# Two layers of a hybrid RWKV-7, attention and Fourier backbone: the recurrence's inverse and key products in other places of the program, with projections put in fixed places between them

## The chip, the cores and the metric

The kernel runs on one core of one Trainium2 chip. The time is device microseconds (us) of one execution, the median of three runs. Beside it stands one profiled execution, which has a time of its own. A core has five engines that run in parallel, each through its own program in order: PE (matrix products; its weight loads are shown as PEld), DVE (elementwise), ACT (activations and copies), POOL (elementwise), and SP, which issues DMA transfers.

## The reference

```python
SEQ, CTX_LEN, D_MODEL, DEPTH = 512, 256, 1024, 2
for l in range(DEPTH):
    a  = modulate(rms_norm(h, norm_mix_pre[l]), m[0], m[1])
    ac = modulate(rms_norm(hc, norm_mix_pre[l]), mc[0], mc[1])
    u_r, u_q, u_k, u_v, u_f, u_g = _split(a @ w_in[l], IN_SIZES)
    c_r, c_q, c_k, c_v, c_f, c_g = _split(ac @ w_in[l], IN_SIZES)
    yr_c, yr, ... = rwkv_branch(c_r, u_r, ...)          # recurrence over 256 context and 512 latent tokens
    ya = windowed_attention(q, k, v, k_c, v_c, attn_sink[l])
    mix = merge_branches(yr, ya, fourier_mix(u_f), u_g, ...)   # gated by sigmoid(u_g)
    h = h + m[2] * rms_norm(mix, norm_mix_post[l])
    ...                                                  # then a gated ConvFFN
def step(S, inp):                                        # the recurrence, both directions, 4 heads of 64
    r_t, w_t, k_t, v_t, kk_t, b_t = inp
    sa = jnp.einsum("bhvk,bhk->bhv", S, -kk_t)
    S = S * w_t[:, :, None, :] + sa[..., :, None] * b_t[..., None, :] + v_t[..., :, None] * k_t[..., None, :]
    return S, jnp.einsum("bhvk,bhk->bhv", S, r_t)
```

## The kernel before, in words

Each of the two layers has a mixing stage (input projection, recurrence, attention, Fourier mixing, gates) and an FFN stage. The change touches the recurrence of the mixing stage and the projections that run beside it.

**Projections.** One projection of 128 columns is three passes of fp32r products over the 1024 inputs (`gemm3`, lines 177, 178, 179 of the kernel before): 24 products over the 512 latent tokens and, where context is wanted, 24 over the 256 context tokens. Layer 0 wants both nearly everywhere, so a projection there is mostly 48 products; in layer 1 most are 24. Its weights come from `wload`: a DMA of `wr`, a rounding to `wh` on ACT, and the rest `wl` on DVE or POOL (line 118); these tiles are rings that turn in the order in which the code asks for them. Besides the nine projections that the recurrence needs there are eight others (K, V, two of Fourier, four of Q, stored to DRAM in `zd`, those of K and Q after a rotation on PE, DVE and POOL), and gate projections, of which `AHEAD` = 12 are asked for ahead of the Fourier part. Their results are in tile `mm`, so `mm` stands for these projections in the rows.

**Recurrence.** The 768 tokens of a layer are cut into 12 chunks of 64, taken in six pairs (w = 0 to 5; 0 and 1 are context), both directions at once. For each pair there are these parts:
- *Features*, `wkv_features`: two low-rank products on PE (line 814), activations on ACT, and scans and products on DVE and POOL (lines 726 to 855), and at its end the *key products* on PE (line 864) with two masks after each (`MR` and `W`, lines 869 and 870 on DVE), and `BK` times a decay on POOL (line 872).
- *Inverse*, `wkv_inverse`: a triangular inverse. Its first part is on DVE: a transpose (909), fifteen rounds of two small operations (917, 919; called the triangle here), and two transposes (929, 930). Its second part, the *merge*, is on PE in five groups of small products (938, 944, 948, 967, 974), with copies on DVE and ACT between them.
- *Two steps*, `wkv_prep` and `wkv_step`: transposes (987, 997), then q0 (1021 and a copy 1024), its product with the inverse (1028, copy 1031 to `XV`), the state's update (1039, and the addition 1042 to `ZV`), and the outputs (1047, 1052).

**Order.** All of the recurrence is emitted in `tc.high_priority()`. The eight other projections and the gates are emitted after it, at lower priority, and a list scheduler puts them on each engine wherever the recurrence leaves room. So in the program before, products of `mm` stand between nearly all groups of the recurrence, and the inverse of the next pair stands on DVE between the operations of the pair before it. After the recurrence comes its readout (`rwkv_readout`), then the Fourier part, with the gates that are left (in layer 0 about 270 products of gates come after the last step, beside the readout).

Of the kernel before, what the change touches and what calls it, by code (L numbers as in the profile page):

```python
# [16 lines left out]
TL = 512  # L17
TC = 256
TT = TL + TC
# [9 lines left out]
ATT_SCALE = 0.125  # L29
# [4 lines left out]
QC = 1152  # L34
KC = QC + 512
VC = KC + 128
FC = VC + 128
# [17 lines left out]
RING = ((5, 3, 3), (8, 4, 6))  # L55

AHEAD = 12
FOUR = 1
RATE = ((1, 1, 0), (1, 1, 1, 2))

# [3 lines left out]
class Kern:  # L64
# [292 lines left out]
    def advance(self, bg, n):  # L357
        for _ in range(n):
            if bg is None or next(bg, self) is self:
                return  # L360

    def gains(self, l, which, G=None, k0=0, n=KD):

        v = 1 if which == "mix" else 4
        row = V_NMIX if which == "mix" else V_NFFN
        if G is None:
            G = self.t(self.cp, [128, KD, 2], f"G{l}{which}")
        self.nc.vector.scalar_tensor_tensor(
            G[:, k0:k0 + n], self.mT[l][:, 8 * v + k0:8 * v + k0 + n], 1.0,
            self.V1[l][:, row + k0:row + k0 + n].unsqueeze(2).broadcast_to((128, n, 2)), ALU.add, ALU.mult)  # L370
        return G, self.mT[l][:, 8 * (v - 1):8 * (v - 1) + 8]
# [406 lines left out]

    def wkv_features(self, l, w, F, P, wp, wt):

        nc = self.nc
        x = P["x"]
        NC = 2
        WT = NC * CH
        W = {}
        MR = self.t(wp, [128, 4 * NC, 128], "MR", bufs=2)
        need_y = l == 0 or w > 1
        m = 128 if need_y else 64
        first = w in (0, 2, 3)
        part = "c" if w < 2 else "l"  # L790
        los = (w * WT, TC - (w + 1) * WT) if w < 2 else ((w - 2) * WT, TL - (w - 1) * WT)
        base = TL if w < 2 else 0

        def rows(t, h):
            return t[64 * h:64 * h + 64]

        for d in range(2):
            lo = base + los[d]

            def flip(s):  # L800
                return s[:, :, ::-1] if d else s
# [29 lines left out]
            e1 = self.t(wp, [128, 2, NC, CH + 1], "e1", bufs=4)  # L831
# [13 lines left out]
            BK = self.t(wp, [128, NC, 2, 128], "BK", bufs=4)  # L845
# [10 lines left out]
            vs = self.t(wp, [128, 2, WT + CH], "vs_", bufs=4)  # L856
            nc.gpsimd.memset(vs[0:64, :, 0:64], 0.0)
            nc.gpsimd.memset(vs[64:128, :, WT:WT + 64], 0.0)
            self.act(vs[0:64, :, 64:64 + WT], tok(F["v"])[0:64])
            self.act(vs[64:128, :, 0:WT], tok(F["v"])[64:128])  # L860
            for h in range(2):
                ps = self.ps()
                for q in range(4):
                    nc.tensor.matmul(ps[:, q * 128:q * 128 + m], lhsT=BK[:, q // 2, q % 2, :],
                                     rhs=W1[h][:, q // 2, q % 2, 0:m], start=True, stop=True)
                pv = ps.rearrange("p (q t) -> p q t", q=4)[:, :, 0:m]
                oth = 1 - h
                mask = lambda z: rows(self.gmask, z)[:, 0:m].unsqueeze(1).broadcast_to((64, 4, m))
                nc.vector.tensor_tensor(rows(MR, h)[:, 4 * d:4 * d + 4, 0:m], rows(pv, h), mask(h), ALU.mult)
                nc.vector.tensor_tensor(rows(W1[h], oth).rearrange("p c k t -> p (c k) t")[:, :, 0:m], rows(pv, oth),  # L870
                                        mask(oth), ALU.mult)
            nc.gpsimd.tensor_tensor(
                BK, BK, e1[:, :, :, 64].rearrange("p k c -> p c k").unsqueeze(3).broadcast_to((128, NC, 2, 128)), ALU.mult)
            W[d] = (W1, BK, vs, e1)
        return w, W, MR, los

    def wkv_scan(self, l, win, then, F, S, wb):
        nc = self.nc
        w, W, MR, los = win
        NC = 2  # L880
        TTt = self.wkv_inverse(MR, wb)
        cur = S["cur"]
        if cur is None:
            cur = self.wkv_prep(0, W, wb)
            for h in range(2):
                nc.gpsimd.memset(cur[0][h][64 * h:64 * h + 64], 0.0)
        for j in range(NC):
            nxt = None
            if j + 1 < NC:
                nxt = self.wkv_prep(j + 1, W, wb)  # L890
            elif then is not None:
                nxt = self.wkv_prep(0, then[1], wb)
            self.wkv_step(l, w, j, F, W, MR, TTt, cur, nxt, wb, los)
            cur = nxt
        S["cur"] = cur

    def wkv_inverse(self, MR, wp):


        nc = self.nc  # L900
        mm = nc.tensor.matmul
        NI = 8
        Fm = self.t(wp, [128, 16, 32], "iv", bufs=3)
        F16 = self.t(wp, [128, 16, 16], "F16", bufs=1)
        T = self.t(wp, [128, 16, 16], "T16", bufs=1)
        tmp = self.t(wp, [128, 64], "itmp", bufs=1)
        m0, m1, r1 = (self.lmask[:, z:z + 1] for z in (0, 1, 2))
# [6 lines left out]
        for q in range(15):  # L914
            n, m = 15 - q, q + 1
# [11 lines left out]
        TTt = self.t(wp, [128, NI, 64], "TTt", bufs=2)  # L927
        Tn = self.t(wp, [128, NI, 64], "iv", bufs=3)
        nc.vector.transpose(Tn.rearrange("q i (b t) -> q t b i", b=4), X2)
        nc.vector.transpose(TTt.rearrange("q i (b t) -> q t b i", b=4), X1)  # L930

        Ps = self.t(wp, [128, NI, 16], "Ps", bufs=1)
        pp = self.ps()
# [41 lines left out]
                   tile_position=(o + 32, o))  # L975
        self.act(TTt[0:32, :, 32:64], pa[1][0:32])
        nc.vector.tensor_copy(TTt[64:96, :, 32:64], pa[1][64:96])
        return TTt

    def wkv_prep(self, j, W, wp):  # L980

# [347 lines left out]
    def mix(self, l, at, atp, W, pls, ring, A, B):  # L1329

        nc, tc, I = self.nc, self.tc, self.I
        ctx = l == 0
        n = TT if ctx else TL
        w_in = I["w_in"][l]
        colw = lambda c: self.wload(w_in[:, c:c + 128])
        rp = self.pool("rp", side=B)
        P = self.rwkv_params(l, rp)
        F = {m: self.t(rp, [128, 2, TT], m) for m in ("r", "k", "v")}
# [7 lines left out]
        for j, c in enumerate(COLS):  # L1346

            wide = ctx or c not in (0, 1, 8)
            if j < len(W):
                pl, pc = pls[j], self.proj(W[j], at, lat=False, ctx=wide)[1]  # L1350
                if j == len(W) - 1 and ring is not None:
                    ring.release()
            else:
                pl, pc = self.proj(colw(c * 128), at, ctx=wide)
# [10 lines left out]
        wa = self.pool("wa", side=B)  # L1365
        wt = self.pool("wt", bufs=6, side=B)
        wb = self.pool("wb", side=B)
        S = {"cur": None}
        with tc.high_priority():
            w0 = self.wkv_features(l, 0, F, P, wa, wt)  # L1370
            w1 = self.wkv_features(l, 1, F, P, wa, wt)
            self.wkv_scan(l, w0, w1, F, S, wb)

        stg = self.pool("stg", bufs=2 + l, side=B)
        cos = self.t(stg, [128, TL], "cos", bufs=1)
        nc.sync.dma_start(out=cos, in_=self.C["c_cos"])
        sin = self.t(stg, [128, TL], "sin", bufs=1)
        nc.sync.dma_start(out=sin, in_=self.C["c_sin"])
        stores = []
        cols = [(KC, 1), (VC, 1), (FC, ctx), (FC + 128, ctx)] + [(QC + 128 * j, ctx) for j in range(4)]  # L1380
        for j, (c, wide) in enumerate(cols):
            t = self.t(stg, [128, TT], "stg")
            pl, pc = self.proj(self.wload(w_in[:, c:c + 128]), at, ctx=wide)
            sc = {} if j < 4 else dict(scale=ATT_SCALE)
            self.act(t[:, :TL], pl, **sc)
            if wide:
                self.act(t[:, TL:], pc[:, :TC], **sc)

            def store(j=j, t=t, m=TT if wide else TL):
                if j == 0 or j > 3:  # L1390
                    self.rope(t, cos, sin, stg)
                nc.sync.dma_start(out=self.zd[l][j, :, :m], in_=t[:, :m])

            stores.append(store)
            if len(stores) > l:
                stores.pop(0)()
        for store in stores:
            store()
        stg.release()


# [49 lines left out]
        work = fill()  # L1451
        with tc.high_priority():
            for w in range(2, 7):
                w0, w1 = w1, self.wkv_features(l, w, F, P, wa, wt) if w < 6 else None
                self.wkv_scan(l, w0, w1, F, S, wb)
            wb.release()
            wt.release()
            wa.release()
            tmp = self.pool("rtmp", side=B)
            self.rwkv_readout(l, F, P, y, tmp)  # L1460
            tmp.release()
# [20 lines left out]
        def back(j, wide=True):  # L1482
            t = self.t(fp, [128, TT], "back", bufs=3)
            m = TT if wide else TL
            nc.sync.dma_start(out=t[:, :m], in_=self.zd[l][j, :, :m])
            return t

        for _ in range(AHEAD):
            self.advance(work, 1)
            self.advance(bg, MODS[l][0])  # L1490
        self.banks(dict(x=3), dict(s=1, v=2, a=1))
# [2 lines left out]
        vt = self.values_layout(back(1), vp)  # L1494
        self.fourier(z, ctx, fp, lambda: (self.advance(work, FOUR), self.advance(bg, MODS[l][1])))
        yf = [pair(t) for t in z]
# [311 lines left out]
```

## Time and profile before

| what | value |
|---|---|
| median of three runs | 2505.8 us (2498.93 to 2506.62) |
| the profiled execution, its own time | 2513.85 us |
| its span in the profile | 2511.9 us |
| PE busy | 2293.3 us, 91% of the span |
| DVE busy | 1889.0 us, 75% |
| ACT, POOL busy | 1052.8 us (42%), 965.1 us (38%) |

All times in rows are from the start of the profiled execution's span. Busy time of an engine in a stretch is time in which at least one of its instructions ran. PEclk is the share of TensorE's full clock (2.4 GHz) that was granted, 0.5 being 1.2 GHz. In layer 0 the recurrence with what lies around it runs from about 143 to 508 us, in layer 1 from about 1539 to 1860 us.

### The profile page before, as it was taken

The page shows a single profiled execution, that of the slowest core. Times are in us where ns is not written, and L with a number is a line of the kernel's source. Part 1 is how long each engine was busy: PE and PEld are TensorE (multiplying, and loading weights), DVE is VectorE, ACT ScalarE, POOL GpSimd, SP SyncE. Part 2 cuts the span into 40 slices and gives each one's busy share as a digit, 9 for nine tenths or more (in the row PEclk, how much of TensorE's full clock was granted, in tenths as well). Part 3 has the DMA queues.
Part 4 walks back from the last instruction along what each step waited for, and adds up shares of the span by engine and source line. Part 5 has one row for each costly group of instructions (what it writes and reads, how often), then busy time and mean ns, then how long its engine had stood idle before and what let it go on. Part 6 is the DMA issues. An engine that isn't in the chain of part 4 may idle for free. (4 is left out here: it accounts for less than half of the span.)

```text
span 2511.9 us, 43604 instructions
## 1 busy us (share of the span) xinstructions
PE 2293.3 (91%) x16612; PEld 1923.1 (77%) x16612; DVE 1889.0 (75%) x3458; ACT 1052.8 (42%) x2153; POOL 965.1 (38%) x965
## 2 busy tenths in 40 slices
PE   7878999999999979999999989889889997899997
PEld 4757777887777768898898777667667776888886
DVE  4967777838866587778778854888667857989988
ACT  3234343335434444343333544435345434544443
POOL 4443322023332363333333544343224424644453
PEclk9989989999999989999999999899999998999999
DMA  7611111644334322222222322112275643322321
GB/s 241 190 51 47 57 37 46 204 146 122 118 122 125 104 67 65 63 72 68 64 69 66 122 93 63 54 59 61 76 211 149 195 128 113 117 88 85 98 89 59
DMA packets 284529, 251.36 MB, mean 100 GB/s; under 512 B 14524, under 2 KB 241300, under 8 KB 284320
## 3 DMA queue, kind: packets, MB, share of 16 engines
q1 hardware_dynamic: 284320, 248.58, 32.0%
q8 instruction: 131, 2.15, 0.4%
q14 instruction: 78, 0.64, 0.1%
HBM read 221.23 MB, written 27.29 MB: 99 GB/s over the span
## 5 line engine op out<-in xcount | busy, mean ns | idle before, releaser
L177 PE MATMUL mm<-at,wh 128*128 128x256 f32 (+2 forms) x1968 | 661.8, 337 | 14.4 <-DVE v L614 7.0
L178 PE MATMUL mm<-at,wh 128*128 128x256 f32 (+2 forms) x1968 | 660.5, 336 | 12.8 <-POOL at L118 7.3
L179 PE MATMUL mm<-at,wl 128*128 128x256 f32 (+2 forms) x1968 | 659.7, 336 | 8.2 <-DVE wl L118 5.9
L118 POOL TENSOR_TENSOR wl<-wr,wh 128x512 fp32r<-128x512 f32 (+1 forms) x248 | 341.8, 1385 | 466.2 <-ACT wh L106 444.0
L177 PEld LDWEIGHTS mm<-at,wh 128*128 128x128 f32 x1968 | 380.8, 194 | 46.9 <-issue 5.6
L178 PEld LDWEIGHTS mm<-at,wh 128*128 128x128 f32 x1968 | 381.1, 194 | 43.4 <-POOL at L118 10.0
L179 PEld LDWEIGHTS mm<-at,wl 128*128 128x128 f32 x1968 | 380.9, 194 | 34.4 <-DVE wl L118 8.9
L106 ACT ACTIVATE wh<-wr 128x512 fp32r<-128x512 f32 (+1 forms) x342 | 204.9, 605 | 235.2 <-PE mm L178 141.3
L118 DVE TENSOR_TENSOR wl<-ws,wh 128x512 fp32r<-128x512 f32 x176 | 166.8, 949 | 65.6 <-ACT wh L106 65.6
L177 PE MATMUL x<-dh,hid 128*128 128x512 f32 x440 | 178.0, 405 | 29.8 <-DVE acc L604 27.7
L295 DVE SCALAR_TENSOR_TENSOR ma<-mw,s,ma 128x256 f32<-128x256 f32 x336 | 187.3, 597 | 11.0 <-DMA mw<-in_mod_w 8.2
L179 PE MATMUL x<-dh,hid 128*128 128x512 f32 x440 | 173.3, 395 | 1.0 <-DVE hid L118 1.0
L178 PE MATMUL x<-dl,hid 128*128 128x512 f32 x440 | 173.2, 394 | 0.0
L604 DVE TENSOR_TENSOR acc<-x,acc 128x512 f32<-128x512 f32 x200 | 134.4, 682 | 24.2 <-PE x L179 23.7
L118 POOL TENSOR_TENSOR dl<-dr,dh 128x1024 fp32r<-128x1024 f32 x44 | 112.2, 2549 | 83.9 <-ACT dh L106 83.9
L106 ACT ACTIVATE wh<-ws 128x512 fp32r<-128x512 f32 x170 | 103.7, 623 | 84.9 <-PE mm L178 70.5
L177 PEld LDWEIGHTS x<-dh,hid 128*128 128x128 f32 x440 | 83.3, 189 | 56.4 <-DVE acc L604 38.6
L154 POOL TENSOR_TENSOR ws<-wr,wr 128x512 f32<-128x512 f32 x42 | 66.4, 1580 | 139.5 <-DVE wl L118 136.9
L178 PE MATMUL x<-at,wh 128*128 128x512 f32 (+2 forms) x312 | 114.4, 367 | 5.0 <-POOL at L118 3.1
L177 PE MATMUL x<-at,wh 128*128 128x512 f32 (+2 forms) x312 | 114.7, 368 | 0.9 <-DVE wh L114 0.7
L106 ACT ACTIVATE P<-P,st 128x513 f32<-128x513 f32 (+5 forms) x120 | 86.0, 722 | 69.8 <-DVE P L1234 58.6
L154 POOL TENSOR_TENSOR ws<-ws,wr 128x512 f32<-128x512 f32 x42 | 62.8, 1495 | 132.5 <-DVE wl L118 75.0
(490 smaller groups left out, 4859.0 us busy)
## 6 DMA issues: line engine op xcount, KB each, us to landing
mw<-in_mod_w SPq DMA_DIRECT2D x96, 512.0 KB, 4.1
wr<-in_ffn_up SPq DMA_DIRECT2D x176, 256.0 KB, 3.1
wr<-in_w_in SPq DMA_DIRECT2D x164, 256.0 KB, 3.0
dr<-in_ffn_down SPq DMA_DIRECT2D x44, 512.0 KB, 3.3
gd<-sg SPq DMA_DIRECT2D x32, 256.0 KB, 2.0
wraw<-in_w_out SPq DMA_DIRECT2D x32, 256.0 KB, 3.7
hd<-h SPq DMA_DIRECT2D x32, 256.0 KB, 2.4
h<-hd SPq DMA_DIRECT2D x28, 256.0 KB, 6.7
```

Source lines behind the costliest of these rows:

```text
L106: return self.nc.scalar.activation(out, in_, func, **kw)
L118: e.tensor_tensor(lo, full, hi.bitcast(F32), ALU.subtract)
L154: e.tensor_tensor(raw[m], raw[x], raw[y], op)
L177: mm(ps, lhsT=lh, rhs=rh, start=first and k == 0, stop=False)
L178: mm(ps, lhsT=lh, rhs=rl, start=False, stop=False)
L179: mm(ps, lhsT=ll, rhs=rh, start=False, stop=last and k == nk - 1)
L295: nc.vector.scalar_tensor_tensor(acc[s], mw[:, k % 4], v, acc[s], ALU.mult, ALU.add)
L604: nc.vector.tensor_tensor(acc[i][:, cs], ps, acc[i][:, cs], ALU.add)
```

## The change

1. `wkv_features` is a generator in two parts: features, and then the key products with their masks and POOL's product. The second part of the next pair runs between the two steps of the current pair (`self.advance(rest, 1)` after j == 0).
2. The inverse of the next pair is emitted right behind the second step of the current pair, ahead of the features of the pair after it.
3. Inside the inverse, between the part on DVE and the merge, `pad()` emits `PADS[l]` other projections (one in layer 0, two in layer 1), ordered on PE behind the newest PE instruction (`issue_after`); the merge is ordered on PE behind them.
4. The eight other projections become a generator that these pads draw from, as do the gates after pair 1; eight (layer 0) or four (layer 1) gates remain for the loop of `AHEAD`. V and Fourier's go ahead of K.

The number of instructions is nearly the same; what moves is their order.

```diff
+PADS = (1, 2)
...
+    def newest(self):
+
+        return next(i for i in reversed(self.nc.cur_bb.bb.instructions) if i.engine == mybir.EngineType.PE)
+
+    def pad(self, work, n):
+
+        with self.tc.issue_after(self.newest()):
+            self.advance(work, n)
...
+            W[d] = (W1, BK, vs, e1)
+        yield w, W, MR, los
+        for d in range(2):
+            W1, BK, _, e1 = W[d]
             for h in range(2):
                 ps = self.ps()
...
-    def wkv_scan(self, l, win, then, F, S, wb):
+    def wkv_scan(self, l, win, then, rest, F, S, wb, pad):
...
-        TTt = self.wkv_inverse(MR, wb)
         cur = S["cur"]
         if cur is None:
+            S["T"] = self.wkv_inverse(MR, wb, pad)
             cur = self.wkv_prep(0, W, wb)
...
+        TTt = S["T"]
...
+            if j == 0:
+                self.advance(rest, 1)
+        if then is not None:
+            S["T"] = self.wkv_inverse(then[2], wb, pad)
         S["cur"] = cur
...
+        pad()
+        with self.tc.issue_after(self.newest()):
+            self.wkv_inverse_merge(MR, TTt, Tn, r1, wp)
+        return TTt
...
+        work = others()
+        with tc.high_priority():
+            f0 = self.wkv_features(l, 0, F, P, wa, wt)
+            w0 = next(f0)
+            self.advance(f0, 1)
+            f1 = self.wkv_features(l, 1, F, P, wa, wt)
+            w1 = next(f1)
+            self.wkv_scan(l, w0, w1, f1, F, S, wb, lambda: self.pad(work, PADS[l]))
+        self.advance(work, 99)
...
             for w in range(2, 7):
-                w0, w1 = w1, self.wkv_features(l, w, F, P, wa, wt) if w < 6 else None
-                self.wkv_scan(l, w0, w1, F, S, wb)
+                f1 = self.wkv_features(l, w, F, P, wa, wt) if w < 6 else None
+                w0, w1 = w1, next(f1) if w < 6 else None
+                self.wkv_scan(l, w0, w1, f1, F, S, wb, lambda: self.pad(work, PADS[l]))
...
-        for _ in range(AHEAD):
+        for _ in range(AHEAD - 4 * PADS[l]):
             self.advance(work, 1)
```

The order of instructions shows where things went. **First place:** PE, layer 0, from the merge of pair 2 to its first step. Before (line 974 is the merge's last group, 987 and 997 the step's transposes, 1028 the first product with the inverse, 1039 the state's update, `mm` other projections):

```order
L974 MATMUL x_3167<-TTt_3073,Pb_3166 32x32
L178 MATMUL mm_4731<-at_291,wh_4721 128x512
L974 MATMUL x_3167<-TTt_3073,Pb_3166 32x32 x15
L987 MATMUL x_3204<-ident_61,vs__441_2507 128x128 x2
L987 MATMUL x_3204<-ident_61,vs__454_2565 128x128 x2
L1028 MATMUL y_3229<-q_539_3238,TTt_3073 64x64
L179 MATMUL mm_4731<-at_290,wl_4722 128x512
L177 MATMUL mm_4731<-at_292,wh_4727 128x512
L997 MATMUL x_3217<-ident_61,BK_2498 128x128 x2
L997 MATMUL x_3217<-ident_61,BK_2556 128x128 x2
L1028 MATMUL y_3229<-q_539_3238,TTt_3073 64x64 x7
...
L1039 MATMUL y_3250<-XV_483_2843,BT_2854 64x64
```

The changed kernel at the same place (its line numbers are shifted: 1005 is the merge's last group, 826 the features' products, 1058 the product with the inverse, 1017 and 1027 the transposes, 880 the key products, 1069 the state's update):

```order
L1005 MATMUL x_3118<-TTt_2956,Pb_3117 32x32 x16
L826 MATMUL x_3160<-xw_667,w_161_645 128x128 x2
L826 MATMUL x_3160<-xa_668,a_162_646 128x128 x2
L1058 MATMUL y_3267<-q_545_3276,TTt_2956 64x64
L826 MATMUL x_3203<-xw_667,w_161_645 128x128 x2
L826 MATMUL x_3203<-xa_668,a_162_646 128x128 x2
L1058 MATMUL y_3267<-q_545_3276,TTt_2956 64x64 x4
...
L880 MATMUL x_3317<-W_514_3156,BK_3185 128x128 x4
L880 MATMUL x_3324<-W_515_3157,BK_3185 128x128 x4
L1069 MATMUL y_3288<-XV_483_2843,BT_2854 64x64
```

The products of `mm` that stood between the groups are gone, and both directions' features (826) and the first direction's key products (880) of the next pair now stand ahead of the update 1069 of the first step. From the merge of pair 2 until the pad behind its second step, PE's program has 76 rows with no `mm` product; the same holds for pairs 3 and 4, and in layer 1.

**Second place:** DVE, layer 0, where the first inverse ends and the second begins. Before (929 and 930 are the last transposes of one inverse, 909 begins the next, 940 to 952 belong to the merge):

```order
L929 STREAM_TRANSPOSE iv_1594<-iv_1588 128x16x4x8
L930 STREAM_TRANSPOSE TTt_1593<-iv_1587 128x16x4x8
L909 STREAM_TRANSPOSE iv_2585<-MR_1431 128x512
L940 COPY Ps_1597<-x_1598 128x128
L912 TENSOR_SCALAR F_458_2586<-iv_2585,table_539 128x256
L913 SCALAR_TENSOR_TENSOR F_458_2586<-iv_2585,table_539,F_458_2586 128x256
L917 TENSOR_TENSOR itmp_2588<-F_458_2586,T_459_2587 128x15
L919 TENSOR_TENSOR T_459_2587<-T_459_2587,itmp_2588 128x15
L917 TENSOR_TENSOR itmp_2588<-F_458_2586,T_459_2587 128x28
L919 TENSOR_TENSOR T_459_2587<-T_459_2587,itmp_2588 128x14x2
L952 SCALAR_TENSOR_TENSOR iv_1594<-x_1598,table_539,iv_1594 32x8x16
L917 TENSOR_TENSOR itmp_2588<-F_458_2586,T_459_2587 128x39
```

The changed kernel, a later pair (950 and 951 are the last transposes, 1054 is q0's copy, 971 to 1008 belong to the merge, 737 and 837 to features):

```order
L950 STREAM_TRANSPOSE iv_3468<-iv_3462 128x16x4x8
L951 STREAM_TRANSPOSE TTt_3467<-iv_3461 128x16x4x8
...
L971 COPY Ps_3539<-x_3540 128x128
L1054 COPY q_616_3787<-y_3778 128x256
L983 SCALAR_TENSOR_TENSOR iv_3468<-x_3540,table_539,iv_3468 32x8x16 x2
L988 COPY TTt_3467<-x_3540 16x8x16
L1001 COPY Pb_3628<-x_3629 32x256
L988 COPY TTt_3467<-x_3540 16x8x16
L1008 COPY TTt_3467<-x_3629 32x8x32
L737 TENSOR_SCALAR wt_3676<-wt_3676 128x256
L837 SCALAR_TENSOR_TENSOR wt_3683<-smask_543,wt_3676 128x256
```

The next pair's triangle no longer stands between the merge's copies; features of the pair after it follow the merge, and the triangle stands whole, behind the masks of the key products.

**Third place:** PE, layer 0, features of the first pair. Before (814 are the features' products, 864 the key products):

```order
L179 MATMUL mm_1916<-at_294,wl_1913 128x512
L177 MATMUL mm_1916<-at_296,wh_1912 128x512
L814 MATMUL x_1319<-xw_667,w_161_645 128x128 x2
L814 MATMUL x_1319<-xa_668,a_162_646 128x128 x2
L178 MATMUL mm_1916<-at_297,wh_1912 128x512
L179 MATMUL mm_1916<-at_296,wl_1913 128x512
...
L177 MATMUL mm_1987<-at_284,wh_1977 128x512
L178 MATMUL mm_1987<-at_285,wh_1977 128x512
L864 MATMUL x_1358<-W_255_1315,BK_1344 128x128 x4
L864 MATMUL x_1365<-W_256_1316,BK_1344 128x128 x4
L179 MATMUL mm_1987<-at_284,wl_1978 128x512
```

Changed (826 and 880 are the same two, and 179 and 180 the pad's projection):

```order
L826 MATMUL x_1326<-xw_667,w_161_645 128x128 x2
L826 MATMUL x_1326<-xa_668,a_162_646 128x128 x2
L826 MATMUL x_1369<-xw_667,w_161_645 128x128 x2
L826 MATMUL x_1369<-xa_668,a_162_646 128x128 x2
L880 MATMUL x_1408<-W_257_1322,BK_1351 128x128 x4
L880 MATMUL x_1415<-W_258_1323,BK_1351 128x128 x4
...
L826 MATMUL x_1443<-xa_668,a_162_646 128x128 x2
L826 MATMUL x_1486<-xw_667,w_161_645 128x128 x2
L826 MATMUL x_1486<-xa_668,a_162_646 128x128 x2
L179 MATMUL mm_1587<-at_284,wh_1577 128x512
L180 MATMUL mm_1587<-at_285,wh_1577 128x512
```

The other projections that ran beside these features are gone from here; in the changed program one projection of 48 products stands ahead of the first merge.

## Rows read from the trace of the kernel before

**Rows 1.** The page: span, and busy time by engine.

```profile
span 2511.9 us, 43604 instructions
...
PE 2293.3 (91%) x16612; PEld 1923.1 (77%) x16612; DVE 1889.0 (75%) x3458; ACT 1052.8 (42%) x2153; POOL 965.1 (38%) x965
```

**Rows 2.** Stretches of layer 0: window, length, busy time by engine (instructions), PEclk, DMA.

```profile
143.00:164.40 21.40, 12.78 (x59) 8.71 (x57) 11.57 (x17) 13.96 (x25) 15.55 (x31) 0.78 0.17 49
164.40:212.40 48.00, 38.39 (x211) 34.30 (x212) 40.71 (x85) 13.51 (x35) 17.93 (x21) 0.88 0.14 47
212.40:257.60 45.20, 41.06 (x577) 33.04 (x579) 33.09 (x83) 20.84 (x55) 17.72 (x31) 1.00 0.14 42
...
354.60:401.80 47.20, 42.99 (x532) 34.70 (x533) 34.26 (x85) 18.27 (x49) 14.31 (x29) 0.82 0.12 35
...
445.60:473.50 27.90, 27.20 (x131) 20.48 (x130) 26.34 (x56) 15.20 (x20) 0.00 (x0) 1.00 0.66 212
...
143.00:508.00 365.00, 329.98 (x3708) 268.89 (x3707) 277.61 (x651) 144.47 (x335) 106.87 (x185) 0.93 0.25 78
```

**Rows 3.** Stretches of layer 0, PE's products of `mm` alone.

```profile
212.40:257.60 45.20, 22.68 (x103) 1.00 0.14 42
...
293.20:302.10 8.90, 8.90 (x51) 1.00 0.32 105
...
164.40:450.00 285.60, 150.77 (x668) 0.93 0.16 52
```

**Rows 4.** Stretches of layer 1, columns as in the second group.

```profile
1538.90:1606.20 67.30, 54.88 (x275) 47.01 (x275) 44.73 (x98) 30.03 (x63) 25.18 (x34) 0.85 0.19 59
...
1696.20:1735.10 38.90, 36.42 (x519) 28.20 (x520) 34.68 (x86) 19.77 (x51) 14.44 (x29) 1.00 0.20 62
1735.10:1775.10 40.00, 37.53 (x523) 28.82 (x524) 35.34 (x87) 19.98 (x52) 14.73 (x29) 1.00 0.20 61
...
1538.90:1860.00 321.10, 287.38 (x3223) 221.75 (x3223) 251.24 (x576) 142.89 (x328) 106.00 (x171) 0.94 0.26 81
```

**Rows 5.** Stretches of layer 1, PE: `mm` alone, and gates in one block.

```profile
1606.20:1815.00 208.80, 106.18 (x347) 0.96 0.19 58
...
1847.80:1860.00 12.20, 12.20 (x56) 1.00 0.73 221
```

**Rows 6.** Line 864 in the whole run: what ended PE's idle time before it.

```profile
  issue: 38.9, 13
  DVE BK L855: 28.8, 15
```

**Rows 7.** DVE's operations from 164.4 to 450 us (six inverses): busy, mean ns, idle before.

```profile
L919 DVE TENSOR_TENSOR T<-T,itmp 128x15 f32<-128x15 f32 (+7 forms) x90 | 21.4, 238 | 2.8
L917 DVE TENSOR_TENSOR itmp<-F,T 128x15 f32<-128x15 f32 (+7 forms) x90 | 20.6, 229 | 2.8
```

**Rows 8.** Timeline of the merge from 312.6 us: start, length, instruction.

```profile
312.61 0.71 PE L938 MATMUL x<-iv,MR 32*32 32x16 f32 x64
...
318.30 0.69 PE L967 MATMUL x<-iv,MR 32*32 32x32 f32 x30
...
322.32 0.69 PE L974 MATMUL x<-TTt,Pb 32*32 32x32 f32 x30
...
323.45 0.42 DVE L977 COPY TTt<-x 32x256 f32<-32x256 f32 x1 [1.72 <-ACT TTt L106]
```

**Rows 9.** PE at half clock: the stretch (columns as before), and a group in it.

```profile
359.90:373.50 13.60, 13.60 (x121) 10.07 (x121) 6.60 (x27) 5.86 (x15) 0.80 (x4) 0.50 0.10 30
...
360.11 1.06 PE L967 MATMUL x<-iv,MR 32*32 32x32 f32 x30
```

**Rows 10.** PE, one pair's features, a step's groups, and its key products.

```profile
374.72 0.38 PE L814 MATMUL x<-xw,w 128*128 128x128 f32 x2
...
380.83 0.69 PE L1039 MATMUL y<-XV,BT 128*64 128x64 f32 x16
...
386.97 1.29 PE L864 MATMUL x<-W,BK 128*128 128x128 f32 x5 [1.34 <-POOL W L853]
```

More of the change, by code (lines that the diff above doesn't have):

```diff
@@ L873, in wkv_features @@
                 BK, BK, e1[:, :, :, 64].rearrange("p k c -> p c k").unsqueeze(3).broadcast_to((128, NC, 2, 128)), ALU.mult)
-            W[d] = (W1, BK, vs, e1)
-        return w, W, MR, los
-    def wkv_scan(self, l, win, then, F, S, wb):
+    def wkv_scan(self, l, win, then, rest, F, S, wb, pad):
         nc = self.nc
@@ L894, in wkv_scan, with wkv_inverse @@
             cur = nxt
+            if j == 0:
+                self.advance(rest, 1)
+        if then is not None:
+            S["T"] = self.wkv_inverse(then[2], wb, pad)
         S["cur"] = cur
-    def wkv_inverse(self, MR, wp):
+    def wkv_inverse(self, MR, wp, pad):
         nc = self.nc
@@ L930, in wkv_inverse, with wkv_inverse_merge @@
         nc.vector.transpose(TTt.rearrange("q i (b t) -> q t b i", b=4), X1)
+        pad()
+        with self.tc.issue_after(self.newest()):
+            self.wkv_inverse_merge(MR, TTt, Tn, r1, wp)
+        return TTt
+    def wkv_inverse_merge(self, MR, TTt, Tn, r1, wp):
+        nc = self.nc
+        mm = nc.tensor.matmul
+        NI = 8
         Ps = self.t(wp, [128, NI, 16], "Ps", bufs=1)
@@ L977, in wkv_inverse @@
         nc.vector.tensor_copy(TTt[64:96, :, 32:64], pa[1][64:96])
-        return TTt
     def wkv_prep(self, j, W, wp):
@@ L1368, in mix @@
         S = {"cur": None}
-        with tc.high_priority():
-            w0 = self.wkv_features(l, 0, F, P, wa, wt)
-            w1 = self.wkv_features(l, 1, F, P, wa, wt)
-            self.wkv_scan(l, w0, w1, F, S, wb)
         stg = self.pool("stg", bufs=2 + l, side=B)
@@ L1378, in mix, with others, store @@
         nc.sync.dma_start(out=sin, in_=self.C["c_sin"])
[L1379 to L1398, printed above, removed]
+        def others():
+            stores = []
+            cols = [(1, VC, 1), (2, FC, ctx), (3, FC + 128, ctx), (0, KC, 1)] + [(4 + j, QC + 128 * j, ctx) for j in range(4)]
+            for j, c, wide in cols:
+                t = self.t(stg, [128, TT], "stg")
+                pl, pc = self.proj(self.wload(w_in[:, c:c + 128]), at, ctx=wide)
+                sc = {} if j < 4 else dict(scale=ATT_SCALE)
+                self.act(t[:, :TL], pl, **sc)
+                if wide:
+                    self.act(t[:, TL:], pc[:, :TC], **sc)
+                def store(j=j, t=t, m=TT if wide else TL):
+                    if j == 0 or j > 3:
+                        self.rope(t, cos, sin, stg)
+                    nc.sync.dma_start(out=self.zd[l][j, :, :m], in_=t[:, :m])
+                stores.append(store)
+                if len(stores) > l or 0 < j < 4:
+                    stores.pop(0)()
+                yield
+            for store in stores:
+                store()
+        work = others()
[7 more added lines that the diff above has]
+        self.advance(work, 99)
         stg.release()
@@ L1453, in mix @@
             for w in range(2, 7):
-                w0, w1 = w1, self.wkv_features(l, w, F, P, wa, wt) if w < 6 else None
-                self.wkv_scan(l, w0, w1, F, S, wb)
+                f1 = self.wkv_features(l, w, F, P, wa, wt) if w < 6 else None
+                w0, w1 = w1, next(f1) if w < 6 else None
+                self.wkv_scan(l, w0, w1, f1, F, S, wb, lambda: self.pad(work, PADS[l]))
             wb.release()
```

## The prediction

> **What bounds the kernel now.** I read the page first: PE is busy 91% of the span and DVE 75% [rows 1], so a change of order can gain at most what PE stands idle, and loses what it makes PE stand idle in addition. Then I read the two stretches that hold the recurrence, window by window. In layer 0, from 143 to 508 us, PE is busy 330.0 of 365.0 us, so it is idle 35 us [rows 2]. In layer 1, from 1538.9 to 1860, it is busy 287.4 of 321.1, idle 34 us [rows 4]. The reader is to see that PE, not the recurrence, sets the pace: one pair lasts 45.2 or 47.2 us in layer 0 with 41.06 and 42.99 us of PE [rows 2], and 38.9 or 40.0 us in layer 1 with 36.42 and 37.53 [rows 4]. DVE has only 33.1 to 34.3 us of work in such a pair in layer 0 and 34.7 to 35.3 in layer 1. PE's time is full because about half of it is other projections: 22.68 of the 41.06 us in the first of those pairs [rows 3].
>
> Where PE does stand idle, it is mostly ahead of the key products (line 864), for the feature tiles W and BK; the two largest entries there are 38.9 and 28.8 us over both layers, with weight loads and products each counted [rows 6]. One pair shows it: the features' products run at 374.7 us, the key products at 387.0, 12 us later, after a wait for W [rows 10].
>
> **What the change does to it, part by part.** The instructions stay the same; what counts is which of them stand between which on PE and DVE. So the sum is one of PE's idle time: new idle minus old idle minus what PE's own work gets shorter.
>
> *The period of a pair without fill.* In pairs 2, 3 and 4 no other projection stands between the merge and the end of the second step. The chain is then one circle: inverse on DVE, merge, features of the next pair, key products, masks, the rest of the steps, inverse again. DVE's queue runs in nearly this order, so the period is DVE's own work plus its waits for PE and ACT that nothing else on DVE covers. DVE's own work is 34 us in layer 0 and about 36 in layer 1, where a pad rounds the weights of two projections. The waits: in the merge, groups of 0.71, 0.69 and 0.69 us [rows 8] with a third to a half microsecond of handing over and copying at each, which I put at 4.5 us; in the second step three groups of about 0.69 [rows 10] with their handing over, 2.7 us; at the start of the features about 1. Together 8.2 us. The triangle used to fill such waits; its thirty operations of 238 and 229 ns, 7 us [rows 7], are now one solid stretch. So a pair takes about 42 us in layer 0, 44 in layer 1. Bounds: 36 us if nearly all waits are covered after all (DVE's largest value of these pairs is 35.3); 48 if PE's groups run at half clock, at which a group of 0.69 us takes 1.06 [rows 8, 9], which makes 12.6 of the 8.2 us, and if DVE loses some more beside POOL.
>
> *PE's work in it.* Without `mm` the first pair has 41.06 - 22.68 = 18.4 us of PE [rows 2, 3]. Counted the other way, 103 products at the pace of a solid block (51 in 8.90 us, 0.175 each [rows 3]) leave 23. I take 20. A pad is 48 products, 8.4 us in layer 0 at that pace, and 10.5 in layer 1 (56 gates of 512 wide in 12.20 us, 0.218 each [rows 5]). So PE is idle 42 - 28.4 = 13.6 and 44 - 30.5 = 13.5 us in such a pair, against 4 now.
>
> *The first features and the first inverse.* Their fill leaves too. Now, to 212.4 us, PE is idle 69.4 - 12.78 - 38.39 = 18 us [rows 2]. Then: the inverse can begin some 8 us earlier, and I put the end of the first merge at 204 us, 61 us from 143, with 12.8 of PE before the key products, 13 of two pairs' features, 8.4 of the pad and 4 of the merge: about 23 idle. In layer 1 the two projections cover more, and 13 are idle, as now (67.3 - 54.88 = 12 [rows 4]).
>
> *The rest of layer 0.* The steps of pair 0 and the second inverse have one projection beside them: 8 idle. Pair 1 gets all other projections that were left, some 270 products, and is bound by PE: 4. Pairs 2 and 3: 27. The steps of pair 4: 10. Pair 5 with its 432 products of gates: 4. Then the readout: now its 27.9 us have PE busy for 27.20 with gates between [rows 2]; in the new order only the Fourier part's small products stand beside it, and I put 20 of the 28 us as idle. Sum 96.
>
> *The rest of layer 1.* By the same steps: 5 for pair 0, 8 for pair 1, 27 for pairs 2 and 3, 11 for the steps of pair 4, 15 for pair 5 and the readout, which keeps 96 gates beside it. With the 13 above: 79.
>
> *What PE saves.* Single products between small groups are dear: 668 in 150.77 us, 0.226 each [rows 3], where a mix of wide and narrow in a block costs 0.2; that is 17 us, of which part overlaps the recurrence's groups. I take 12, with bounds of 0 and 34 (down to 0.175). In layer 1 347 cost 106.18 us, 0.306 each, against 0.218 [rows 5]: 30 us at most; but 20 us of recurrence and some 72 products at 0.218 already make 35.7 of the 36.4 to 37.5 us busy in a pair, so I take 8.
>
> *Sum.* Layer 0: 96 - 35 - 12 = 49. Layer 1: 79 - 34 - 8 = 37. Together 86 us slower. Against the profiled execution's 2513.85 us that is 2600; it lies 8 us above the median of the runs, which I take as the base: 2505.8 + 86 = 2592.
>
> *What the key products' new place does.* It can't take the wait of 12 us away: the next features' first products (826 in the changed kernel) stand behind the merge on PE, so the features begin there, and the first direction's key products stand ahead of the first step's update on PE's queue. The update, the state and everything behind them now wait for features of the pair to come; before, only other projections stood behind that wait. That wait is inside the 42 us, since DVE computes the features in it.
>
> *Clock.* The granted clock was 0.50 for 13.6 us in a pair of layer 0 while PE was busy all of that time, with narrow and small groups after an idle stretch, and 0.82 over that pair [rows 2, 9]. The new stretches without fill have more idle time, so half clock in part of them is likely; I leave it out of the sum and keep it as a rival. The Trainium skill (TensorE: Matmul & The Clock Gate, section HAM oscillation) says that short bursts of products with waits between them fall back to the half clock again and again; by that rule the case with slow groups would hold in each pair, and the time would be that of the second rival below.
>
> **The rivals.** *First, the other side: the interleaving itself is the cost.* If the lone products' price is wholly given back (34 + 30 instead of 20: -44), the pairs fall to 36 us (6 us for three pairs' worth in each layer: -36), and Fourier's products cover the readout (20 to 8, 15 to 6, and 23 to 16 at the start: -28), the sum is 86 - 108 = -22: 2484 us. For it speaks the 0.306 of layer 1; against it that PE's busy time of a pair there holds only about 1 us of surplus. It decides from pairs shorter than about 36 us with the readout covered.
>
> *Second, half clock in all stretches without fill.* Pairs of 48 us: 6 us for three pairs' worth in each layer, +36, and 10 more at the first features and the readout: 86 + 46 = 132, 2638 us. For it speaks the stretch at 0.50; against it that the pads are solid blocks, after which the clock was 1.00 [rows 3].
>
> *Third, nothing comes of it:* what is idle in pairs 2 to 4 is idle instead of the waits ahead of line 864, and the rest is as before: 2506 us. Against it stands that these waits are only 4 us a pair.
>
> **How the numbers follow.** I give the forecast 0.64, the first rival 0.12, the second 0.15, and the third 0.09. A measurement of this kernel tells about 0.3% (7.5 us) from no change. Of the third rival half lies within that, the rest is slower by little: faster 0.12, same 0.05, slower 0.83. The bounds of the terms reach from 86 - 36 - 44 = 6 to 86 + 36 + 20 + 20 (nothing saved, and 20 more in the stretches that I placed by hand) = 162. The range from 2508 to 2660 leaves out the first rival and part of the third below, and a little of the second above.
>
> **What would show it.** In the new profile PE's busy time falls by some 20 us, and its idle time in each of the two stretches more than doubles. The merges of pairs 2, 3 and 4 follow each other at 42 to 44 us, with some 13 us of PE idle in each, mostly ahead of the key products (880) and in the merge. The largest fall of layer 0 should lie behind pair 5, with the readout bare. The prediction is wrong if merges follow each other at 36 us or less, if features are done before the merge ends, or if the other projections of pair 1 leave that stretch so much shorter that the idle time is won back there.

## The result, and the profile after

The changed kernel takes 2648.2 us (median of four runs, 2646.5 to 2650.9), against 2506.2 us for the kernel before: 1.0572 times as long, 95% interval 1.0547 to 1.0597. That is 142 us more where 86 were forecast. The profiled execution took 2646.65 us; the one before had taken 2513.85, 8 us over its median, so the two profiles are 133 us apart and not 142.

The page of the changed kernel (span, busy time by engine), which answers to [rows 1]:

```profile
span 2644.7 us, 43673 instructions
...
PE 2348.2 (89%) x16612; PEld 1972.0 (75%) x16612; DVE 1890.4 (71%) x3458; ACT 1054.9 (40%) x2153; POOL 955.3 (36%) x965
```

The span grew by 132.8 us. PE's busy time grew by 54.9 us for the same instructions, and its idle time by 77.9 (2644.7 - 2348.2 = 296.5 against 218.6). So there are two losses, and one of them, more busy time, had been forecast with the other sign.

Both lie in the two mixing stages. These are their stretches, from the features to about the same place behind the attention, with the columns of [rows 2], first before (layer 0, layer 1), then after:

```profile
143.00:855.00 712.00, 666.65 (x5841) 546.73 (x5839) 494.63 (x1132) 288.53 (x647) 216.23 (x282) 0.96 0.32 98
1538.90:2083.00 544.10, 495.53 (x4469) 384.67 (x4468) 406.25 (x893) 243.59 (x540) 191.81 (x245) 0.96 0.37 112
...
139.00:946.00 807.00, 713.29 (x5851) 578.62 (x5851) 496.51 (x1135) 287.54 (x646) 215.67 (x282) 0.91 0.28 86
1628.80:2216.00 587.20, 509.58 (x4482) 406.99 (x4482) 403.69 (x892) 246.38 (x541) 185.76 (x244) 0.91 0.34 104
```

PE's idle time grew by 48 us in layer 0 and 29 in layer 1, its busy time by 47 and 14. The granted clock fell from 0.96 to 0.91 in both. Over the whole span PE was busy at 1.2 GHz for 141.5 us before and for 239.5 after (the spans of its instructions laid over the clock records of the two traces).

The first features of layer 1 show how the loss is shared. They began at 1538.9 us before and at 1628.8 after (timeline of PE, before and after):

```profile
1538.94 0.71 PE L814 MATMUL x<-xw,w 128*128 128x128 f32 x4
```

```profile
1628.79 0.71 PE L826 MATMUL x<-xw,w 128*128 128x128 f32 x4 [0.35 <-DVE kk L782]
```

So some 90 us were lost up to there, with layer 0, and 43 from there on.

Stretches of layer 0 of the changed kernel, cut at the merges (line 969), with the columns of [rows 2]; behind them two pairs of layer 1, as in [rows 4]:

```profile
139.00:192.60 53.60, 22.02 (x124) 18.16 (x124) 41.22 (x93) 23.82 (x52) 24.80 (x45) 0.75 0.09 28
192.60:234.10 41.50, 35.67 (x504) 29.84 (x504) 23.08 (x62) 12.49 (x33) 9.23 (x23) 0.71 0.01 2
234.10:318.80 84.70, 83.36 (x795) 69.08 (x794) 43.42 (x99) 28.60 (x66) 31.34 (x43) 1.00 0.25 80
318.80:363.90 45.10, 33.50 (x483) 28.84 (x482) 33.41 (x81) 16.64 (x47) 12.82 (x28) 0.81 0.07 22
363.90:408.70 44.80, 35.01 (x497) 30.00 (x496) 33.37 (x82) 16.48 (x47) 13.94 (x28) 0.77 0.07 22
408.70:469.40 60.70, 49.31 (x593) 42.60 (x592) 38.19 (x90) 17.02 (x42) 10.16 (x16) 0.89 0.10 30
469.40:563.00 93.60, 93.47 (x652) 66.02 (x652) 11.99 (x26) 18.00 (x38) 2.65 (x3) 0.88 0.28 87
563.00:600.00 37.00, 28.62 (x110) 19.59 (x109) 29.15 (x63) 13.94 (x19) 2.84 (x3) 0.88 0.46 150
...
1782.80:1828.60 45.80, 35.05 (x485) 29.42 (x485) 34.00 (x83) 17.85 (x49) 12.92 (x28) 0.85 0.10 30
1828.60:1875.70 47.10, 37.08 (x501) 30.94 (x504) 34.51 (x84) 17.77 (x49) 13.95 (x28) 0.82 0.13 40
```

The reader is to see three things. The pairs without fill last 45.1 and 44.8 us, and 45.8 and 47.1 in layer 1. PE is idle in them for 9.8 to 11.6 us, but busy for 33.5 to 37.1, at a granted clock of about 0.8. And the stretch from 469.4 to 563.0, which holds the last pair's merge and steps and nearly six gates, has PE busy all the time; it holds 276 products of `mm`, and lasts 94 us.

### The profile page after: what moved, and what is told of

It reads as the page before. It is cut to its first block, busy times and chain, and to the rows that moved or that the text cites. A ratio compares the mean times of both kernels' runs of the same rounds, so it can differ in the third digit from the quotient of the medians.

```text
span 2644.7 us, 43673 instructions
## 1 busy us (share of the span) xinstructions
PE 2348.2 (89%) x16612; PEld 1972.0 (75%) x16612; DVE 1890.4 (71%) x3458; ACT 1054.9 (40%) x2153; POOL 955.3 (36%) x965
## 5 line engine op out<-in xcount | busy, mean ns | idle before, releaser
L120 DVE TENSOR_TENSOR wl<-wr,wh 128x512 fp32r<-128x512 f32 x96 | 75.1, 786 | 74.5 <-ACT wh L108 68.1
```

The source lines that it names most:

```text
L120: e.tensor_tensor(lo, full, hi.bitcast(F32), ALU.subtract)
```

## The experiments

Each time is a median; each ratio is to the kernel before, with its 95% interval. Together they split the change into its parts (first five runs), its tail (two), and the pair without fill (the rest). The expectations name four theories: A, only the missing fill costs; B, the new places lengthen a pair by themselves; C, single products between small groups are dear; D, DVE's queue sets the period of a pair.

**The control.** The inverse back at the start of its pair, the key products directly behind their features, and no pads (the edit is shortened here and below):

```diff
-PADS = (1, 2)
+PADS = (0, 0)
-            if j == 0:
-                self.advance(rest, 1)
-        if then is not None:
-            S["T"] = self.wkv_inverse(then[2], wb, pad)
+        S["T"] = self.wkv_inverse(MR, wb, pad)      # at the start of wkv_scan
...
-        with self.tc.issue_after(self.newest()):
-            self.wkv_inverse_merge(MR, TTt, Tn, r1, wp)
+        self.wkv_inverse_merge(MR, TTt, Tn, r1, wp)
```

> The control for the three runs without pads: inverse at the start of its pair, key products straight behind their features, no pads. What is left of the change is that the eight other projections come in the order V, Fourier, Fourier, K, Q instead of K, V, Fourier, Q. If those runs measure the moves, this one is the kernel before: 2498 to 2517 us. If the order of projections carries part of their loss: 2520 us or more.

Measured: 2505.1 us, 0.9992 (0.9971 to 1.0013). The order of the projections costs nothing that shows, so the next three runs measure the moves alone.

**Key products moved, nothing else** (the control with `self.advance(rest, 1)` back between the steps):

> Only the key products of the next pair between the two steps; the inverse stands at the start of its own pair as before, and no pads. Theory A: within 0.5% of the kernel before, 2494 to 2520 us, since other projections stand behind the key products again. Theory B: over 2530 us, since the first step's state waits for the next pair's features on PE's and DVE's queues, whatever fill there is.

Measured: 2574.5 us, 1.0263 (1.0228 to 1.0298). The wait of PE ahead of the merge from 201 to 411 us in this kernel, and the same entry of the kernel before from 212 to 402 us and of the control from 210 to 390 (us in total, times, longest):

```profile
PE x L966 <- DVE iv L948: 33.0, 5, 10.8
```

```profile
PE x L938 <- DVE iv L929: 0.5, 1, 0.5
```

```profile
PE x L964 <- DVE iv L946: 4.0, 1, 4.0
```

The wait ahead of the key products, 10.1 us in the kernel before, is gone, and a longer one stands ahead of the merge: the masks now come after the first step, so the inverse on DVE begins later and is not ready when the merge wants it. Theory A, that only the missing fill costs, had this within 0.5% and is wrong here. The wait is not the whole loss: the profile has some 40 us more of idle PE than the control's, and some 28 us more of busy PE (2329.0 against 2300.5), at a granted clock of 0.82 in these pairs against 0.90.

**The inverse moved, nothing else** (the control with the inverse of the next pair behind the second step):

> Only the inverse's new place, behind the second step of the pair before; key products directly behind their features as before, no pads. Theory A: 2495 to 2525 us. Theory B, if it is the inverse that lengthens the circle: over 2540 us.

Measured: 2544.9 us, 1.0149 (1.0114 to 1.0184), 20 us past theory A's range and just within theory B's. Here the merges of layer 0 go from 208.2 to 426.7 us, those of the control from 210.1 to 408.4. The first four gaps together are no longer (173.0 us against 180.1), the last one is, 45.5 us instead of 18.2. In the old place the last pair's inverse was computed while the pair before it was at its merge and steps. How much of the 37 us this is stays open: in the longer gap PE is busy for 40.2 us, 22.1 of them with other projections, of which the control's last gap has 9.4.

**Both moves, no pads:**

> Inverse and key products stay in their new places, but no projection is emitted between the inverse's two parts, nothing is ordered behind anything on PE, and all twelve gates are asked for after the recurrence, as before. Theory A (the fixed places take the fill away from the recurrence, that is all): 2495 to 2525 us, PE busy at most 2305 us, merges 40 to 50 us apart. Theory B (the new places of inverse and key products lengthen the circle of a pair by themselves): above 2560 us.

Measured: 2563.3 us, 1.0218 (1.0176 to 1.0260), just above theory B's bound. So the moves cost some 55 us although other projections can still go anywhere, and the pads with their fixed order the other 85 or so, to 2648.

**Pads and the early inverse, key products directly behind their features:**

```diff
             w1 = next(f1)
+            self.advance(f1, 1)
-            if j == 0:
-                self.advance(rest, 1)
```

> The changed kernel with its pads and the early inverse, but the key products emitted straight behind their features. Theory A (the pads' fixed order costs, the key products' place little): 2630 to 2655 us. If the key products between the steps hold up the first step's state (theory B): pairs shorter by 2 us or more, below 2625 us.

Measured: 2699.7 us, 1.0764 (1.0719 to 1.0809). Neither expectation held. With the pads, the key products between the steps help: without that move a pair lasts 45.9 and 49.9 us and the kernel is 51.5 us slower. The parts don't add up: without the pads the same move, on top of the early inverse, costs 18 us (2563.3 against 2544.9).

**The tail in one block** (layer 0, all nine projections that are left go ahead of the last pair's merge):

```diff
-                self.wkv_scan(l, w0, w1, f1, F, S, wb, lambda: self.pad(work, PADS[l]))
+                self.wkv_scan(l, w0, w1, f1, F, S, wb, lambda w=w: self.pad(work, 9 if l == 0 and w == 5 else PADS[l]))
...
         for _ in range(AHEAD - 4 * PADS[l]):
-            self.advance(work, 1)
+            if l:
+                self.advance(work, 1)
```

> The changed kernel, but in layer 0 the eight gates that ran beside the last pair stand in one block ahead of its merge, so that nothing alternates with the last pair's small products, and the last pair and the readout are bare. Theory C (in layer 0's tail 132 single products between groups of two small ones cost about 28 us more than in a block): 28 us saved, about 18 us lost on bare PE, so 2630 to 2645 us, with PE busy 2315 to 2325 instead of 2348 us. If the alternation is not what costs there: 2655 us or more, and PE busy over 2335 us.

Measured: 2628.6 us, 1.0481 (1.0439 to 1.0523), PE busy 2328.0 us: nearest theory C, with the time just below its range and the busy time just above. What the tail looked like in the changed kernel shows in PE's timeline there:

```profile
500.22 0.21 PE L979 MATMUL x<-TTt,Ps 32*16 32x16 f32 x2
500.36 0.50 PE L180 MATMUL mm<-at,wh 128*128 128x512 f32 x1
500.79 0.21 PE L979 MATMUL x<-TTt,Ps 32*16 32x16 f32 x2
```

One wide product and two small ones take 0.57 us in turn, where a wide one takes 0.218 in a block [rows 5]. The clock was full here, and fell later on, with no idle time on PE ahead of it (PE alone: length, busy, PEclk, DMA):

```profile
499.40:501.40 2.00, 2.00 (x11) 1.00 0.16 46
...
511.40:527.40 16.00, 16.00 (x74) 0.50 0.14 44
```

The merge and the steps of the last pair stood so from 495.7 to 563.0 us. In the tail block's kernel the same work, from the fifth merge to the end of the steps, takes 136 us with 119.7 of PE busy:

```profile
408.00:522.30 114.30, 103.46 (x881) 90.32 (x880) 44.55 (x99) 31.56 (x70) 13.69 (x19) 0.91 0.24 74
522.30:544.00 21.70, 16.19 (x377) 13.47 (x376) 5.42 (x16) 4.85 (x13) 1.84 (x2) 0.60 0.42 135
```

In the changed kernel it is 154.3 us with 142.8 busy (the two rows from 408.7 to 563.0 above).

**Three projections in every pad,** `PADS = (3, 3)`:

> The changed kernel with three projections in every pad of both layers, so that all twelve gates stand in blocks and none is left to run beside the last pair or the readout. Theory C (single products between small groups are dear, blocks are not): PE busy falls to 2330 us or below, and layer 0 ends no later than in the changed kernel; layer 1's pairs get longer by what a pad exceeds the inverse on DVE, some 5 us each; 2625 to 2655 us in all. If it is PE's bareness in the tail that decides: 2670 us or more.

Measured: 2635.8 us, 1.0511 (1.0466 to 1.0555); PE busy 2337.6 us, a little over the bound. The last pair's steps in layer 0 end 27 us earlier than in the changed kernel, at 535 us instead of 562, and layer 1 begins 26 us earlier:

```profile
1602.70 1.04 PE L826 MATMUL x<-xw,w 128*128 128x128 f32 x4
```

Layer 1 then takes 12 us longer. Blocks everywhere are better than the alternating tail, but the pairs stay as bare as they were.

**DVE's part in the pair without fill** was tried from two sides. First, the rest of the gates' weights on POOL:

```diff
-lo_engs=("dve" if E["tag"] == "mm" else "pool",)
+lo_engs=("pool",)
```

> The changed kernel with the rest of the gates' weights (wl) computed on POOL instead of DVE while the recurrence runs. Theory D (in a pair without fill, DVE's queue is the circle: its 33.4 us of work and its waits make the 45): two operations of 0.69 us and their wait of 1.6 us leave DVE, merges stand 42 to 43 us apart, 2615 to 2640 us. If the circle is PE's: merges stay 45 us apart, 2642 to 2655 us.

Measured: 2654.8 us, 1.0596 (1.0570 to 1.0622). The merges stand 43.9 and 45.0 us apart, nearer to the second expectation than to theory D's 42 to 43. DVE's waits from 315.7 to 404.6 us tell why so little came of it:

```profile
DVE Ps L971 <- PE x L969: 8.4, 2, 6.0
DVE MR L885 <- PE x L880: 4.7, 2, 2.4
DVE wt L737 <- ACT wt L108: 3.4, 2, 1.8
```

DVE was done earlier and then waited up to 6.0 us for the merge's first products, which are queued on PE behind the pad. Pad and inverse end at nearly the same time, and either of them can hold up the merge. In the changed kernel itself it is the pad: the inverse's last transpose ends at 362.30 us, and PE runs pad products without a break until the merge begins 1.6 us later (the next pair: 407.24 and 408.71).

```profile
361.22 1.08 DVE L951 STREAM_TRANSPOSE TTt<-iv 128x512 f32<-128x512 f32 x1
...
363.89 0.73 PE L969 MATMUL x<-iv,MR 32*32 32x16 f32 x64
```

Second, the features of one direction behind the first step (the generator's `yield` moved to the end of `d == 0`), against the wait that is PE's largest in these pairs. From 318.8 to 408.7 us in the changed kernel:

```profile
PE y L1077 <- DVE ZV L1072: 10.7, 4, 4.3
```

> The changed kernel with the second direction's features of the next pair emitted behind the current pair's first step, so that the state's addition (ZV) of that step no longer queues on DVE behind them; PE waits 4.3 to 4.7 us for it in each pair now. Theory D (DVE's work and waits make the circle, PE's wait is only where it shows): merges stay 43 to 47 us apart, 2625 to 2665 us. If that wait itself lengthens the pair: merges 41 us apart or less, below 2620 us.

Measured: 2662.6 us, 1.0633 (1.0606 to 1.0661), with merges 43.4 and 44.4 us apart. PE's wait for ZV went, and one of about the same length stands ahead of the key products (324.4 to 412.2 us):

```profile
PE x L881 <- DVE BK L867: 9.1, 2, 4.7
...
PE y L1078 <- DVE ZV L1073: 2.1, 2, 1.0
```

The wait moved with the order on DVE's queue, and the period stayed within 1.7 us in layer 0 (in layer 1 the merges stand 48.5 and 47.7 us apart, against 45.8 and 47.1). That is within theory D's ranges. It shows that this wait did not set the period; after the run on POOL it does not show that DVE alone does.

**The clock** took three attempts. In the changed kernel's pair at 318.8 us, PE alone (length, busy, PEclk):

```profile
335.30:338.30 3.00, 0.70 (x17) 1.00 0.00 0
338.30:339.80 1.50, 0.00 (x0) 0.99 0.00 0
339.80:341.30 1.50, 0.10 (x2) 0.50 0.00 0
341.30:344.30 3.00, 3.00 (x36) 0.50 0.02 5
```

PE waits for ZV, and comes out of the wait at 1.2 GHz. The second key products, which the masks on DVE wait for (second line: 2.4 us in each of the two pairs), then take 3.60 us for sixteen:

```profile
343.30 3.60 PE L880 MATMUL x<-W,BK 128*128 128x128 f32 x16
...
DVE MR L885 <- PE x L880: 4.7, 2, 2.4
```

The first attempt put extra products into the state update's own tile, ahead of the update and ahead of the first step's outputs:

> The changed kernel with 4 wide extra products ahead of each state update and 12 half-wide ones ahead of the first step's outputs, where PE waits for ZV; their results are overwritten and serve nothing. Rival 2 (half clock makes a pair without fill longer): PEclk of these pairs rises from 0.8 to over 0.9, merges stand 41 to 43 us apart instead of 45, and the time falls to 2615 to 2635 us. If the clock isn't what sets the pair: merges stay 45 us or more apart, 2645 to 2670 us.

Measured: 2688.5 us, 1.0728 (1.0674 to 1.0782); PEclk 0.85, merges 47.9 and 47.8 us apart. The second put more of them there and some into the merge's tile:

> The changed kernel with extra products whose results are overwritten: 32 half-wide ones (3.5 us at full clock) where PE waits for ZV, and some 0.7 us ahead of each of the merge's last two groups. Rival 2's mechanism (half clock lengthens the circle): the second key products take 2.0 us instead of 3.6 and PEclk over a pair rises from 0.8 to over 0.9; merges 41 to 43.5 us apart; 2615 to 2640 us. If the clock is not on the circle: PEclk rises, but merges stay at 45 us; 2645 us or more.

Measured: 2712.4 us, 1.0825 (1.0787 to 1.0863); PEclk 0.83, merges 49.3 and 51.2 us apart. Both say nothing of the clock, since the extra products waited for ZV themselves, whose reading of that tile they have to follow; from 328.4 to 428.9 us in the second (1082 are the extra products):

```profile
PE y L1082 <- DVE ZV L1078: 8.2, 2, 4.1
```

They show at most that products which themselves wait for ZV lengthen the pair. The third attempt has a tile of its own:

```diff
+    def spin(self, n):
+        with self.tc.issue_after(self.newest()):
+            ps = self.ps("mm")
+            for _ in range(n):
+                self.nc.tensor.matmul(ps, lhsT=self.AT[0][0][:, 0:128], rhs=self.AT[0][0][:, 0:512], start=True, stop=True)
```

> The changed kernel with extra products into a tile of their own that nobody reads, so that they wait for nothing: 16 wide ones (3.5 us at full clock) behind the first step's state update, where PE waits for ZV, and three in each of the merge's two last waits. It is the pairs without fill that count here, pairs 2 to 4 of both layers; in the others PE has no idle time and the products cost up to 5 us a pair. Rival 2's mechanism (half clock lengthens the circle): the second key products take some 2.1 us instead of 3.6, PEclk of these pairs rises from 0.8 to over 0.9, and their merges stand 41 to 43.5 us apart instead of 45. If the clock is not on the circle: PEclk rises and merges stay 44.5 us or more apart.

Measured: 2645.4 us, 1.0546 (1.0502 to 1.0589). Three pairs of layer 1 and two of layer 0, and the second key products of the first:

```profile
1778.20:1821.50 43.30, 36.45 (x507) 29.82 (x506) 33.86 (x83) 17.94 (x49) 12.67 (x28) 0.96 0.11 33
1821.50:1865.60 44.10, 37.23 (x519) 30.48 (x518) 34.91 (x84) 17.80 (x49) 13.43 (x28) 0.96 0.12 37
1865.60:1914.10 48.50, 42.80 (x523) 34.87 (x524) 35.95 (x88) 15.72 (x41) 10.51 (x16) 0.82 0.12 37
330.30:375.20 44.90, 37.99 (x507) 31.15 (x506) 32.94 (x81) 16.67 (x47) 12.87 (x28) 0.85 0.07 22
375.20:419.60 44.40, 38.92 (x523) 32.13 (x523) 33.50 (x82) 16.61 (x47) 13.94 (x28) 0.85 0.07 23
...
1800.66 2.05 PE L886 MATMUL x<-W,BK 128*128 128x128 f32 x16
```

The third of these pairs in the changed kernel:

```profile
1875.70:1923.00 47.30, 34.73 (x500) 29.09 (x499) 36.39 (x88) 15.59 (x41) 10.39 (x16) 0.86 0.10 29
```

In two pairs of layer 1 the clock rose to 0.96, and they are 2.5 and 3.0 us shorter than in the changed kernel, although PE does some 5 us of useless work in each. In the third the clock did not rise (0.82, before 0.86), and it is 1.2 us longer. In layer 0 the clock only rose to 0.85, still half in the features, and the pairs are 0.2 and 0.4 us shorter. So the first expectation is met, or missed by 0.6 us, only where the clock rose. Half clock does lengthen the circle, by 2.5 to 3 us where it could be removed; the kernel's time did not change by more than its runs differ.

## Why the prediction was right, and where its sum was off

The direction held, the range held, and the main reason held for the larger part: PE lost its fill in the recurrence, and the fixed pads cost some 85 of the 142 us. The forecast of 86 us was too small by 56 in the medians and 47 in the profiles, and the term that failed is **"What PE saves"**. It took 12 and 8 us off for single products that would stand in blocks. In fact PE's busy time rose by 55 us, a miss of 75 in that term; the idle time was over-counted (78 instead of 96 - 35 + 79 - 34 = 106). These two misses partly cancel, so it is in part luck that the total came out nearer than its terms.

- *Where the busy time came from.* In the tail of layer 0, singles were not gathered into blocks; some 130 were dealt out one by one between small products, mostly pairs. The sum took these products and the last pair as a bulk, whatever their order. The block in their place took away 20 us, both of time and of PE's busy time. The rest is what half clock can account for: a pair without fill was put at 28.4 and 30.5 us of PE and has 33.5 to 37.1, and PE was busy at 1.2 GHz for 98 us more than before. At the price of the groups seen at both levels (1.06 against 0.69 us [rows 8, 9], 3.60 against 2.05) that is an estimated 34 to 42 us; no run takes it away as a whole.
- *The period.* 42 and 44 us were forecast; 45.1, 44.8, 45.8 and 47.1 came. That DVE's queue makes most of the circle fits the moved features, but is not shown: the pad is as long as the inverse and ends after it in both pairs of layer 0, so it holds the merge, which I had not seen. In the first two pairs of layer 1 the surplus is the clock's, shown by the third attempt, whose pairs at 0.96 last 43.3 and 44.1. In the third pair, and in layer 0, how much is the clock's stays open.
- *The second rival* (half clock, 2638 us) came nearest to the measured time, 10 us below it. The rule of the Trainium skill that I set beside it (TensorE: Matmul & The Clock Gate, section HAM oscillation) agrees with the rows: the clock fell to 0.50 in the long wait shown above and stayed there for the small products behind it. But the rival put the whole surplus into the period, at 48 us, and that was not it.
- *The moves themselves.* The prediction gave them no cost beside the lost fill. The runs without pads show 37, 66 and 55 us (ratios of 1.0149, 1.0263 and 1.0218 on 2507) for the inverse, the key products and both. So 55 of the 142 us are no lost fill of fixed places. For the key products the larger part of the new idle time is shown: the merge waits for its inverse, 33.0 us in four gaps of layer 0. For the inverse the longer last gap is shown, but not what it costs.
- *The key products' wait* could not be taken away, as forecast; it became the wait for ZV, 10.7 us in two pairs. The prediction also read too much into that wait: the 38.9 us in [rows 6] is an entry without a releaser ("issue"), only the 28.8 us names BK, and of the 12 us in [rows 10] PE was idle for 1.34.
- *The readout* was less bare: 8.4 us idle from 563 to 600 us, not 20, because Fourier's products filled it. PE's longest idle time of layer 0 is ahead of the first merge, 31.6 of 53.6 us where 23 were forecast; what the tail lost lay in pair 5, with PE busy.

## What to carry to other kernels

A product that is placed by hand fills one gap and leaves the others: before fixing an order, list every wait of the loop and what covers it, and ask which of those covers the fixed place takes away. When work is moved, look at the order it leaves behind at the far end as well, down to single instructions: a turn of one wide product and two small ones cost more than twice here what the wide one costs in a block. And moving a consumer of a queue (features, a state's addition) may only move the wait, as it did here.

## What the runs showed of the hardware

A wide product that alternates with two products of 32 rows has a turn of 0.57 us at a granted clock of 1.00, against 0.218 us in a block. In that alternation the granted clock fell to 0.50 for 16 us (511.4 to 527.4 us) although PE was busy without a break. And idle time on PE was not free: products that nobody needed, some 5 us a pair, made two pairs of layer 1 shorter by 2.5 and 3.0 us; the key products behind the wait then ran at 2.4 GHz (2.05 us for sixteen, against 3.60 after a wait in layer 0).
